# Opening fillers, five groups of squares, a reordered even mixer and shorter boundary sums in a two-layer decoder trunk

## The chip, the cores and the metric

The kernel runs on one core of one Trainium2 chip, in one launch. The metric is device time in microseconds (us). Five engines work beside each other and are tied by semaphores: PE (TensorE, matrix products), DVE (VectorE), ACT (ScalarE), POOL (GpSimd) and SP (SyncE, which here only starts transfers). Each runs its own instructions strictly in the order in which they stand in its program, so an instruction that waits holds up all that stand behind it on that engine.

## The reference, cut to what matters

A trunk of two layers over 512 tokens of width 1024, conditioned by a vector `c`. Layer 0 has the even mixer (sliding-window attention and a Conformer convolution side by side), layer 1 a state-space mixer. Each mixer and each feed-forward block is preceded by an RMS norm and a modulation, so that the sum of squares over the width of `x` is needed at the start, at three places between blocks, and at the end.

```
silu_c = silu(c)
for i in range(2):
    sh_m, sc_m, g_m, sh_f, sc_f, g_f = split(silu_c @ w_mod[i] + b_mod[i], 6)
    h = rmsnorm(x, norm_mix[i]) * (1 + sc_m) + sh_m
    y = even_mixer(h, ...) if i == 0 else ssd_mixer(h, ...)
    x = x + g_m * y
    h = rmsnorm(x, norm_ffn[i]) * (1 + sc_f) + sh_f
    x = x + g_f * ((silu(causal_conv(h @ w_gate)) * (h @ w_val)) @ w_down)
return rmsnorm(x, final_norm)          # x * rsqrt(mean(x*x) + eps) * g
```

In the even mixer, `q`, `k`, `v` and the convolution's input are `h @ w_in + b_in`; `q` and `k` are rotated by angles worked out from `positions`; the attention's and the convolution's outputs are joined and multiplied by `w_out`.

## The kernel before, in words

`x` lies transposed: eight tiles of 128 channels (`kt`), each 128 partitions by 512 tokens. Every fp32 product is made as three products of rounded halves (`mm3`, L370 to L372): high by high, low by high, high by low. So a weight tile is cast on ACT to its high part (`head`, L317 `wh`) and its remainder is subtracted on DVE (`rest`, L322 `wl`); the weights of the first projection that share the opening have their own cast (L753, `wg_head`) and remainder (L757, `wg_rest`), and the activation `hn` likewise an `upper` part (L790, ACT) and a `lower` one (L794, DVE).

**Opening.** The eight tiles of `x` are squared on ACT (L693). DVE adds the first seven squares into one tile (`x_add`, L696), and PE sums that tile and the eighth square over the partitions by products with a column of ones (`x_sum`, L702, four products of one column for each tile). PE also spreads constants (L404) and runs ten filler products, `warm` (L672). The root (ACT L728), Newton's step (DVE L425 to L429) and a spread of the result (`x_row`, L404) follow; then the first tile of `hn` is made, and `begin` (L798) starts the first projection, six banks wide, with `hh`, `hl` and `lh` products for each `kt` as the tiles come. The modulation's dot products run on DVE meanwhile (`mod_dot`, L595, an operation of 128x1024). POOL works out the rotary angles (L1279 on), and then starts eight small transfers.

**Even mixer.** The rest of the projection (eight column tiles of 24 products each), the Conformer's convolution as PE products (L950), scores (mask L1041 and L1048), the transposes of the probabilities (L1090), their copies to SBUF on ACT (L1097, `bring`), the products with V (L1108) and the products with `w_out` are all tasks of one plan. A list scheduler orders them by the length of the chain behind a task plus a weight from a table by the task's name (`MIXER0`); the result is a fixed order on every engine.

**Boundary.** The function that closes a block works in two halves of 256 tokens (`hf` 0 and 1). For each output tile: products, `residual` (DVE L474), its square on ACT (L501), and, as long as more tiles follow, an addition of an older square into `acc` on DVE (L499). When the last tile of half 0 is done, `W.ahead()` prepares one weight tile of the next block (cast on ACT, remainder on DVE), and `norm_steps` sums `acc` and the squares that were not yet added by products with ones (L396: six products of 128x1 for a half), then takes the root (ACT L508) and Newton's step (DVE L510 to L516). There are four such places: after the even mixer, after each feed-forward block and after the state-space mixer; the last one has no weight left to prepare, and `final` multiplies and writes the output.

Of the kernel before, what the change touches and what calls it, by code (L numbers as in the profile page):

```python
# [24 lines left out]
P = 128  # L25
# [45 lines left out]
WARM = 10  # L71
# [7 lines left out]
MIXER0 = {'sigmoid': 150, 'square': -128, 'osq_add': -45, 'head': 130, 'tap0': -113, 'attn_h': 63, 'conv_h': -48, 'out_c': -99, 'gated': -114, 'rest': -119, 'values': 58, 'rope': 138, 'rstd': -10, 'mod_sum': 7, 'attn_l': 143, 'var': 124, 'turn': -64, 'mod_end': -110, 'exp': -57, 'bring': -43, 'conv_sum': 54, 'out_a': -120, 'osq': 8, 'mod_act': -104, 'mod_add': 39, 'mod_free': 120, 'normalize': 150, 'load': -64, 'product': -72, 'mean_row': -150, 'mod_dve': 105, 'tap': -30, 'recip': -56, 'ln': -15, 'centre': -64, 'residual': 71, 'maxima': 147, 'rstd_row': 38, 'conv_l': -16, 'mean': 47, 'rope_in': 128, 'v_bias': 31, 'mod_load': -56, 'mod_dot': -129, 'root': -125, 'rows': -16, 'rows_in': 47, 'v_turn': -18, 'v_in': 45, 'mod 2': -83, 'head 0': 40, 'mu': 146, 'keys': -96, 'conv 0': 150, 'head 1': -134, 'mod 1': -150, 'head 3': -150, 'shifts': -98, 'scores': -50, 'mod 0': 117, 'conv 3': -14, 'conv 2': 11, 'cbias': 86, 'conv': 82, 'store': 86, 'taps': 79, 'conv 1': 84, 'head 2': -150, 'wg_load': 80, 'c_row': -142, 'norm': 96, 'hl': -96, 'x_newton': -58, 'preload': 145, 'others': -120, 'wg_head': 62, 'finish': 115, 'sines': 150, 'v_load': -81, 'first 4': 88, 'upper': 126, 'wg_rest': 138, 'hh': -129, 's_gain': 79, 'first 2': -68, 'widen': -150, 'x_load': 72, 'x_root': -38, 'x_add': -61, 'x_total': -33, 's_dot': 38, 'lh': 105, 'x_sq': 80, 'masks': 73, 't_turn': 145, 'c_in': -110, 'ss_load': -128, 'first 5': -56, 'gain': 115, 'w_free': -14, 'normed': 104, 'margins': -50, 'side': -136, 'x_row': 146, 'first 0': 11, 'h_dot': 129, 't_in': -51, 'first 1': -141, 'first 6': -43, 'angles': -150, 'first 3': -16, 'lower': 49, 'first 7': -17, 'h_bias': 25, 'x_sum': -40, 'late': -140, 'late0': 65, 'csum': 55, 'warm': -93, 'p_dot': 70, 'p_in': 4, 'p_sum': 43, 'mean_in': 100}  # L79
# [145 lines left out]
def trunk(ctx: ExitStack, tc: tile.TileContext, xT_d, vecs_d, rows_d, dsk_d, pos_d, const_d, wss_d, wg0_d,  # L225
# [250 lines left out]
    def boundary(ws, ms, acts, gate, acc, nxt, after=None):  # L476
# [28 lines left out]
        def norm_steps(hf):  # L505
            s_ = token_sums([acc[:, HALF[hf]], *sq[hf]], 2)
            sd, v, y_, a, y2 = (small(2) for _ in range(5))
            act(sd, s_, AF.Sqrt, scale=1.0 / 1024.0, bias=eps[:, 0:1])  # L508
            yield
            ts(v, s_, 1.0 / 1024.0, 1e-6, ALU.mult, ALU.add)  # L510
            nc.vector.reciprocal(y_, sd)
            tt(a, y_, y_, ALU.mult)
            yield
            stt(a, a, -0.5, v, ALU.mult, ALU.mult)
            yield
            stt(y2, a, 1.5, y_, ALU.add, ALU.mult)  # L516
            yield
            y[hf] = spread(y2, 2)
# [126 lines left out]
    def even_layer(lp, cp, dp0):  # L645
# [49 lines left out]
        def x_add(k):  # L695
            tt(st["xq", 0], st["xq", 0], st["xq", k], ALU.add)  # L696
# [8 lines left out]
        sums = None  # L705
# [104 lines left out]
        for kt in range(KT):  # L810
# [5 lines left out]
            wl_ = add("wg_rest", "DVE", 0.93, lambda kt=kt: wg_rest(kt), [wh_], None, dict(raw=1))  # L816
# [1001 lines left out]
    def final(fp):  # L1818
        def fill(hf, rb):
# [144 lines left out]
```

## Time and profile before

| | |
|---|---|
| median of 3 runs | 1341.47 us (1340.62 to 1342.1) |
| the profiled execution | 1342.0 us |
| its span, first to last instruction | 1340.2 us |
| PE busy | 1313.2 us, 98% of the span |
| DVE, ACT, POOL busy | 875.1, 597.0, 74.7 us |
| mean granted TensorE clock | 0.990 |
| share of PE in the chain that ended last | 93% |

The profile has a page for the whole execution (busy time of each engine, the span in forty slices, the chain of work that ended last, the costliest groups) and views of a stretch: a timeline of single instructions or runs of like ones, a table of busy times and granted clock by stretch, and the waits of one engine. A granted clock of 1.00 is 2.4 GHz and 0.50 is 1.2 GHz. An instruction is named by its line in the kernel before.

### The profile page before, as it was taken

Reading aid. Unit: us, or ns where it says so; the run is one execution under the profiler, and the core shown is the slowest. Engines: PE = TensorE matmul, PEld = TensorE weight load, DVE = VectorE, ACT = ScalarE, POOL = GpSimd, SP = SyncE. Lnnn points to the kernel's source line nnn. Section 1 sums busy time; section 2 is a strip of 40 time slices with the busy share of each in tenths; the row PEclk is TensorE's granted clock in tenths of the full one; section 3 lists DMA queues with packets and bytes.
Section 4 is the critical chain, followed back from the end, with each engine's and each line's share of the span. In section 5 each row is a group of like instructions: output and inputs, shape, how many; then the busy total and the mean of one; then the engine's idle time right before and its main releaser. Section 6 shows DMA issues by size and latency. Waiting matters only on the chain.

```text
span 1340.2 us, 17613 instructions
## 1 busy us (share of the span) xinstructions
PE 1313.2 (98%) x6873; PEld 1078.0 (80%) x6873; DVE 875.1 (65%) x1342; ACT 597.0 (45%) x947; POOL 74.7 (6%) x129
## 2 busy tenths in 40 slices
PE   7999899999999999999999999999999999999997
PEld 6856589888888888897888887887988888888886
DVE  6976987775666676568686775878665434434443
ACT  4624734432233233347694764836353313322333
POOL 7010000000000000100110100000000000000002
PEclk8999899999999999999999999999999999999999
DMA  9773363564664665223542432342223233233311
GB/s 341 236 266 103 128 210 111 170 222 152 215 194 149 218 203 180 89 68 95 166 139 84 139 110 97 122 123 79 64 94 115 89 111 94 83 92 112 99 56 63
DMA packets 56436, 183.64 MB, mean 137 GB/s; under 512 B 7008, under 2 KB 10144, under 8 KB 56352
## 3 DMA queue, kind: packets, MB, share of 16 engines
q1 hardware_dynamic: 51536, 170.24, 39.5%
q0 software_dynamic: 4128, 11.61, 2.6%
q8 instruction: 54, 0.88, 0.3%
q10 hardware_dynamic: 688, 0.66, 0.1%
q14 instruction: 30, 0.25, 0.1%
HBM read 179.21 MB, written 3.28 MB: 136 GB/s over the span
## 4 chain that ended last, share of the span: by engine, by line
PE 93%; DVE 3%; ACT 2%; DMA 1%; issue 1%; DVEq 0%; ACTq 0%; POOLq 0%
PE ps L370 27%; PE ps L371 27%; PE ps L372 27%; PE ps L798 2%; PE ps L950 2%; PE ps L1643 1%; DMA M<-scr 1%; PE ps L1621 1%; PE ps L404 1%; PE ps L396 1%; PE ps L1609 1%; ACT M L1593 0%; PE ps L419 0%; PE ps L1108 0%; PE ps L1635 0%
## 5 line engine op out<-in xcount | busy, mean ns | idle before, releaser
L370 PE MATMUL ps<-hn,wh 128*128 128x512 f32 (+1 forms) x1214 | 460.2, 379 | 0.8 <-ACT hn L461 0.8
L371 PE MATMUL ps<-hn,wh 128*128 128x512 f32 (+1 forms) x1214 | 454.1, 374 | 0.4
L372 PE MATMUL ps<-hn,wl 128*128 128x512 f32 (+1 forms) x1214 | 453.9, 374 | 0.0
L322 DVE TENSOR_TENSOR wl<-raw,wh 128x1024 fp32r<-128x1024 f32 (+1 forms) x208 | 250.9, 1209 | 95.1 <-ACT wh L317 93.8
L317 ACT CAST wh<-raw 128x1024 fp32r<-128x1024 f32 (+1 forms) x208 | 213.1, 1027 | 221.5 <-PE ps L371 216.1
L370 PEld LDWEIGHTS ps<-hn,wh 128*128 128x128 f32 x1214 | 228.5, 188 | 44.6 <-issue 3.5
L371 PEld LDWEIGHTS ps<-hn,wh 128*128 128x128 f32 x1214 | 228.7, 188 | 42.3 <-issue 1.9
L372 PEld LDWEIGHTS ps<-hn,wl 128*128 128x128 f32 x1214 | 228.5, 188 | 40.7
L474 DVE SCALAR_TENSOR_TENSOR x<-ps,modv,x 128x512 f32<-128x512 f32 (+1 forms) x108 | 73.9, 690 | 115.2 <-PE ps L372 115.2
L370 PE MATMUL ps<-fh,wh 128*128 128x512 f32 (+1 forms) x380 | 142.2, 374 | 0.0
L371 PE MATMUL ps<-fl,wh 128*128 128x512 f32 (+1 forms) x380 | 141.9, 373 | 0.0
L372 PE MATMUL ps<-fh,wl 128*128 128x512 f32 (+1 forms) x380 | 141.9, 373 | 0.0
L595 DVE SCALAR_TENSOR_TENSOR mr<-mr,cb 128x1024 f32<-128x1024 f32 x92 | 111.1, 1219 | 1.6 <-DMA mr<-in_wmod_dram 1.6
L1346 ACT ACTIVATE tmp<-ps,vecs 128x512 f32<-128x512 f32 x44 | 34.2, 777 | 114.8 <-PE ps L372 114.8
L1347 DVE SCALAR_TENSOR_TENSOR tmp<-ps,vecs,tmp 128x511 f32<-128x511 f32 x44 | 32.9, 749 | 79.6 <-ACT tmp L1346 79.6
L370 PEld LDWEIGHTS ps<-fh,wh 128*128 128x128 f32 x380 | 71.5, 188 | 12.8
L372 PEld LDWEIGHTS ps<-fh,wl 128*128 128x128 f32 x380 | 71.5, 188 | 12.7
L371 PEld LDWEIGHTS ps<-fl,wh 128*128 128x128 f32 x380 | 71.5, 188 | 12.6
L295 ACT CAST fh<-tmp 128x512 fp32r<-128x512 f32 x44 | 27.3, 620 | 96.4 <-DVE tmp L1351 95.6
L449 POOL TENSOR_TENSOR ssq<-ssq,tmp 128x512 f32<-128x512 f32 x10 | 13.4, 1337 | 909.8 <-ACT tmp L448 909.8
L1349 ACT ACTIVATE tmp<-tmp 128x512 f32<-128x512 f32 x44 | 27.8, 632 | 75.6 <-DVE tmp L1348 75.5
L1593 ACT ACTIVATE M<-M,acs 128x128 f32<-128x128 f32 x128 | 39.6, 389 | 24.4 <-DMA M<-scr 24.3
(291 smaller groups left out, 1462.1 us busy)
## 6 DMA issues: line engine op xcount, KB each, us to landing
raw<-in_w_dram SPq DMA_DIRECT2D x176, 512.0 KB, 3.7
mr<-in_wmod_dram SPq DMA_DIRECT2D x80, 512.0 KB, 3.7
raw<-in_w_dram SPq DMA_DIRECT2D x32, 448.0 KB, 3.4
mr<-in_wss_dram SPq DMA_DIRECT2D x16, 512.0 KB, 7.2
M<-scr POOLq DMA_DIRECT2D x16, 512.0 KB, 4.6
s<-uc SPq DMA_DIRECT2D x16, 266.0 KB, 5.2
raw<-in_wg_dram SPq DMA_DIRECT2D x8, 384.0 KB, 7.5
E<-scr POOLq DMA_DIRECT2D x32, 96.0 KB, 3.7
```

What stands on the lines that cost most here:

```text
L295: nc.scalar.copy(h, src)
L317: nc.scalar.copy(h, self.raw[i].rearrange("p (k m) -> p k m", m=P))
L322: eng.tensor_tensor(l, self.raw[i].rearrange("p (k m) -> p k m", m=P), h.bitcast(F32), ALU.subtract)
L370: mm(ps, lhsT=w[0], rhs=ah, start=first, stop=False)
L371: mm(ps, lhsT=w[0], rhs=al, start=False, stop=False)
L372: mm(ps, lhsT=w[1], rhs=ah, start=False, stop=last)
L474: stt(x[:, m, hs], ps, gate(m), x[:, m, hs], ALU.mult, ALU.add)
L595: stt(raw, raw, 1.0, mod_pool[2], ALU.mult, ALU.mult, accum_out=out)
L1346: act(c, pg, AF.Identity, bias=vec("fcb", i), scale=vec("fcw", 3 * i + 2))
L1347: stt(c[:, 1:], pg[:, :T - 1], vec("fcw", 3 * i + 1), c[:, 1:], ALU.mult, ALU.add)
L1349: act(c, c, AF.Silu)
L1593: act(m_[:, i, c, :], m_[:, i, c, :], AF.Relu, bias=acs[:, c, h:h + 1], scale=-1.0)
```

## The change

It has seven parts.

1. Eight filler products (`warm`), now of a column of ones with itself, stand at the head of PE's program; seven more stand between the sums of the squares, and the first `hh` product waits for all of them.
2. The squares of `x` are summed on PE in five groups (tile 0; tile 1; tiles 2 to 5, which DVE adds with three additions; tile 6; tile 7) instead of two, so twenty one-column products instead of eight, and three additions instead of six.
3. The angles on POOL are held until the upper part of tile 4 of `hn` is there, by a small copy from it that POOL makes first.
4. The opening's remainders (`wg_rest`) may go to DVE or to POOL.
5. The table `MIXER0` has other weights, so that the whole even mixer is ordered anew.
6. `norm_steps` adds left-over squares into `acc` on DVE first, until none is left in half 0 and one in half 1: two products with ones in half 0 and four in half 1, instead of six in each.
7. The last output transfers leave from other queues: the last tile's from ACT's instead of SP's, and the first pair of tiles of the second half goes one step earlier.

The core of the diff (the table's numbers are left out, the order below tells what they do):

```diff
-WARM = 10
+WARM, EARLY = 7, 8
+ANGLES_AT = 4
...
         def norm_steps(hf):
+            while len(sq[hf]) > hf:
+                tt(acc[:, HALF[hf]], acc[:, HALF[hf]], sq[hf].pop(0), ALU.add)
             s_ = token_sums([acc[:, HALF[hf]], *sq[hf]], 2)
...
+        filler = ones.broadcast_to([P, P])
         def warm():
-            mm(g0[NG0 - 1][:, 0:P], lhsT=ident, rhs=con[:, :P], start=True, stop=True)
+            mm(g0[NG0 - 1][:, 0:P], lhsT=filler, rhs=filler, start=True, stop=True)
+        for _ in range(EARLY):
+            warm()
...
         def x_add(k):
-            tt(st["xq", 0], st["xq", 0], st["xq", k], ALU.add)
+            tt(st["xq", 2], st["xq", 2], st["xq", k], ALU.add)
...
-            if k == 0:
-                sums = t
-            elif k < KT - 1:
-                sums = add("x_add", "DVE", 0.69, lambda k=k: x_add(k), [t, sums], None, dict(tmp=1))
-            else:
-                sums = add("x_sum", "PE", 1.0, lambda: x_sum(0), [sums], dict(ps=1), dict(tmp=1))
+            if 2 < k < 6:
+                added = add("x_add", "DVE", 0.69, lambda k=k: x_add(k), [t, added], None, dict(tmp=1))
+            if k == 2:
+                added = t
+            elif k in (0, 1):
+                sums = add("x_sum", "PE", 1.0, lambda k=k: x_sum(k), [t, sums], None if k else dict(ps=1), dict(tmp=1))
+            elif k == 5:
+                sums = add("x_sum", "PE", 1.0, lambda: x_sum(2), [added, sums], None, dict(tmp=1))
+            elif k > 5:
                 sums = add("x_sum", "PE", 1.0, lambda k=k: x_sum(k), [t, sums], None, dict(tmp=1))
+        warms = []
         for _ in range(WARM):
-            add("warm", "PE", 0.45, warm, cbs)
+            warms.append(add("warm", "PE", 0.45, warm, [], bonus=-400))
...
-            wl_ = add("wg_rest", "DVE", 0.93, lambda kt=kt: wg_rest(kt), [wh_], None, dict(raw=1))
+            wl_ = plan.either("wg_rest", [Way("DVE", 0.93, lambda kt=kt: wg_rest(kt, nc.vector)),
+                                          Way("POOL", 1.75, lambda kt=kt: wg_rest(kt, nc.gpsimd))],
+                              [wh_], None, dict(raw=1))
...
-                hh = add("hh", "PE", 1.39, lambda kt=kt: begin(kt, 0, 0), [wh_, h_, begun])
+                hh = add("hh", "PE", 1.39, lambda kt=kt: begin(kt, 0, 0), [wh_, h_, begun, *(() if kt else warms)])
-                angles_at = hh if kt == 2 else angles_at
+                angles_at = h_ if kt == ANGLES_AT else angles_at
...
         def angle():
+            nc.gpsimd.tensor_copy(small(8), hn[ANGLES_AT][0][:, 0:8].bitcast(F32))
...
                 tt(o[:, kt % 2, :], x[:, kt, hs], rb, ALU.mult)
+                if hf and n == 5:
+                    nc.scalar.dma_start(out_d[:, 0:2, hs], os_[0])
                 if hf and n > 3:
-                    nc.sync.dma_start(out_d[:, kt:kt + 1, hs], o[:, kt % 2:kt % 2 + 1, :])
+                    (nc.scalar if n == 5 else nc.sync).dma_start(out_d[:, kt:kt + 1, hs], o[:, kt % 2:kt % 2 + 1, :])
...
-            nc.scalar.dma_start(out_d[:, 0:2, hs], os_[0])
+            if not hf:
+                nc.scalar.dma_start(out_d[:, 0:2, hs], os_[0])
```

How the order changes, at three places (lines of the changed kernel stand a few higher: L672 becomes L676, L702 L709, L404 L405, L774 L785, L322 L323, L474 L475).

PE at its start, before: two spreads of constants (`con`), ten fillers, two groups of sums (`ones,tmp`).

```order
L404 MATMUL ps_134<-con 128x128 x4
L404 MATMUL ps_144<-con 128x128 x4
L672 MATMUL ps_126<-con 128x128 x10
L702 MATMUL ps_194<-ones,tmp_139 128x1 x4
L702 MATMUL ps_194<-ones,tmp_178 128x1 x4
L774 MATMUL ps_208<-mr_169,con 32x128 x8
L404 MATMUL ps_237<-con,sm_225 128x128 x4
```

PE at its start in the changed kernel:

```order
L676 MATMUL ps_126<-ones 128x128 x8
L405 MATMUL ps_142<-con 128x128 x4
L405 MATMUL ps_152<-con 128x128 x4
L709 MATMUL ps_162<-ones,tmp_147 128x1 x4
L676 MATMUL ps_126<-ones 128x128
L709 MATMUL ps_162<-ones,tmp_150 128x1 x4
L676 MATMUL ps_126<-ones 128x128 x3
L709 MATMUL ps_162<-ones,tmp_159 128x1 x4
```

Fillers now stand ahead of everything and between the sums. Two more groups follow (`tmp_188`, `tmp_193`), each behind one filler, then L785 as before, the last filler, and the spread of the root.

DVE at the first boundary, half 0, before: residuals (L474), additions of squares (L499), the remainder of the weight tile that is prepared ahead (L322), Newton's step (L510 on).

```order
L474 SCALAR_TENSOR_TENSOR x<-ps_2024,modv,x 128x256
L499 TENSOR_TENSOR ssq_129<-ssq_129,tmp_2022 128x256
L474 SCALAR_TENSOR_TENSOR x<-ps_2041,modv,x 128x256
L322 TENSOR_TENSOR wl_2066<-raw_2057,wh_2065 128x1024
L510 TENSOR_SCALAR sm_2106<-ps_2098 128x2
L511 RECIPROCAL sm_2107<-sm_2105 128x2
```

The same place in the changed kernel:

```order
L475 SCALAR_TENSOR_TENSOR x<-ps_2040,modv,x 128x256
L500 TENSOR_TENSOR ssq_137<-ssq_137,tmp_2038 128x256
L475 SCALAR_TENSOR_TENSOR x<-ps_2057,modv,x 128x256
L323 TENSOR_TENSOR wl_2082<-raw_2073,wh_2081 128x1024
L508 TENSOR_TENSOR ssq_137<-ssq_137,tmp_2055 128x256
L508 TENSOR_TENSOR ssq_137<-ssq_137,tmp_2071 128x256
L513 TENSOR_SCALAR sm_2120<-ps_2116 128x2
```

The two new additions (L508) stand behind the remainder, and PE's two products with ones (L397, which read `ssq_137`) wait for the second of them. The second and third boundary read the same.

POOL behind its first memsets, before: the angles follow at once.

```order
L653 MEMSET zeros 128x30
L662 MEMSET s_117 128x512
L662 MEMSET s_119 128x512
L1279 CAST sm_392<-pos 128x4
L1282 ISA
L1282 TENSOR_TENSOR ang_394<-sm_392,invf 128x32
```

POOL in the changed kernel:

```order
L656 MEMSET zeros 128x30
L665 MEMSET s_117 128x512
L665 MEMSET s_119 128x512
L768 ISA
L768 TENSOR_TENSOR wl_233<-raw_205,wh_232 128x768
L768 TENSOR_TENSOR wl_318<-raw_288,wh_317 128x768
L768 TENSOR_TENSOR wl_410<-raw_373,wh_409 128x768
L887 COPY sm_441<-hn_438 128x8
L1293 CAST sm_443<-pos 128x4
```

Three remainders (of tiles 0, 2 and 4) and the holding copy now stand ahead of the angles.

## Rows read from the trace of the kernel before

**Rows 1.** The page: busy time by engine; share of the chain that ended last.
```profile
PE 1313.2 (98%) x6873; PEld 1078.0 (80%) x6873; DVE 875.1 (65%) x1342; ACT 597.0 (45%) x947; POOL 74.7 (6%) x129
...
PE 93%; DVE 3%; ACT 2%; DMA 1%; issue 1%; DVEq 0%; ACTq 0%; POOLq 0%
```

**Rows 2.** PE's waits: for whom; total us, times, longest.
```profile
PE ps L1108 <- ACT s L1097: 4.1, 3, 3.3
PE ps L1643 <- DVE M L1600: 3.5, 3, 1.7
```

**Rows 3.** Timeline of PE, opening: start, us, engine, line, operands, [idle before, releaser].
```profile
4.63 3.78 PE L404 MATMUL ps<-con 128*128 128x128 f32 x16 [4.63 <-ACT con L657]
8.21 3.20 PE L672 MATMUL ps<-con 128*128 128x128 f32 x20
13.82 1.95 PE L702 MATMUL ps<-ones,tmp 128*128 128x1 f32 x16 [2.42 <-DVE tmp L696]
...
17.00 2.08 PE L404 MATMUL ps<-con,sm 128*128 128x128 f32 x8 [0.66 <-DVE sm L429]
...
21.26 2.93 PE L798 MATMUL ps<-hn,wh 128*128 128x512 f32 x6 [0.96 <-ACT hn L790]
...
24.27 2.86 PE L798 MATMUL ps<-hn,wl 128*128 128x512 f32 x6
...
27.63 1.67 PE L798 MATMUL ps<-hn,wh 128*128 128x512 f32 x6
```

**Rows 4.** Windows: PE, PEld, DVE, ACT, POOL busy, granted clock, DMA share, GB/s.
```profile
20.00:25.00 5.00, 4.04 (x18) 3.06 (x11) 3.44 (x5) 1.92 (x6) 4.31 (x10) 0.50 1.03 405
152.00:154.00 2.00, 0.14 (x2) 0.00 (x0) 2.00 (x4) 1.09 (x2) 0.00 (x0) 1.00 0.85 281
164.00:166.00 2.00, 2.00 (x6) 1.57 (x5) 2.00 (x3) 2.00 (x12) 0.00 (x0) 0.50 0.05 8
...
900.00:910.00 10.00, 8.33 (x52) 6.69 (x51) 3.89 (x5) 9.08 (x22) 0.32 (x1) 1.00 0.27 78
```

**Rows 5.** Opening's last square (ACT), remainder (DVE line), a POOL addition, sines (ACT).
```profile
6.73 4.07 ACT L693 ACTIVATE tmp<-x 128x512 f32<-128x512 f32 x6 [0.99 <-DMA x<-in_xT_dram]
...
L757 DVE TENSOR_TENSOR wl<-raw,wh x8: 946/958/965, 16.9 to 47.8; 128x768 fp32r<-128x768 f32 x8
...
L449 POOL TENSOR_TENSOR ssq<-ssq,tmp x10: 1286/1298/1535, 554.1 to 1318.9; 128x512 f32<-128x512 f32 x10
...
65.20 0.35 ACT L878 ACTIVATE ang<-ang 128x32 f32<-128x32 f32 x2
```

**Rows 6.** Timeline of PE at the attention's end.
```profile
145.21 1.13 PE L1048 MATMUL ps<-s,s 64*128 64x256 f32 x8
...
155.48 1.15 PE L1108 MATMUL ps<-s,s 128*64 128x128 f32 x12 [3.34 <-ACT s L1097]
...
157.90 2.08 PE L1048 MATMUL ps<-s,s 64*128 64x256 f32 x8
```

**Rows 7.** Timeline of ACT, PE and DVE, first boundary; the addition's line, min/median/max ns.
```profile
211.69 1.03 ACT L317 CAST wh<-raw 128x1024 fp32r<-128x1024 f32 x1
...
212.00 0.50 PE L396 MATMUL ps<-ones,ssq 128*128 128x1 f32 x4
...
212.75 1.23 DVE L322 TENSOR_TENSOR wl<-raw,wh 128x1024 fp32r<-128x1024 f32 x1 [1.48 <-ACT wh L317]
...
213.26 0.37 PE L370 MATMUL ps<-s,wh 128*128 128x256 f32 x1
...
L499 DVE TENSOR_TENSOR ssq<-ssq,tmp x8: 415/418/426, 208.3 to 963.0; 128x256 f32<-128x256 f32 x8
```

**Rows 8.** Timeline of the tail: DVE's outputs, last issues of ACT and SP.
```profile
1333.24 2.08 DVE L1828 TENSOR_TENSOR o<-x,ps 128x256 f32<-128x256 f32 x6 [1.21 <-ACT rs L1822]
...
1334.72 0.44 ACTq L1834 DMA_DIRECT2D out_dram<-o  x1
1335.15 1.52 SPq L1830 DMA_DIRECT2D out_dram<-o  x2
```

More of the change, by code (lines that the diff above doesn't have):

```diff
@@ L78 @@
 N_S = 26
-MIXER0 = {'sigmoid': 150, 'square': -128, 'osq_add': -45, 'head': 130, 'tap0': -113, 'attn_h': 63, 'conv_h': -48, 'out_c': -99, 'gated': -114, 'rest': -119, 'values': 58, 'rope': 138, 'rstd': -10, 'mod_sum': 7, 'attn_l': 143, 'var': 124, 'turn': -64, 'mod_end': -110, 'exp': -57, 'bring': -43, 'conv_sum': 54, 'out_a': -120, 'osq': 8, 'mod_act': -104, 'mod_add': 39, 'mod_free': 120, 'normalize': 150, 'load': -64, 'product': -72, 'mean_row': -150, 'mod_dve': 105, 'tap': -30, 'recip': -56, 'ln': -15, 'centre': -64, 'residual': 71, 'maxima': 147, 'rstd_row': 38, 'conv_l': -16, 'mean': 47, 'rope_in': 128, 'v_bias': 31, 'mod_load': -56, 'mod_dot': -129, 'root': -125, 'rows': -16, 'rows_in': 47, 'v_turn': -18, 'v_in': 45, 'mod 2': -83, 'head 0': 40, 'mu': 146, 'keys': -96, 'conv 0': 150, 'head 1': -134, 'mod 1': -150, 'head 3': -150, 'shifts': -98, 'scores': -50, 'mod 0': 117, 'conv 3': -14, 'conv 2': 11, 'cbias': 86, 'conv': 82, 'store': 86, 'taps': 79, 'conv 1': 84, 'head 2': -150, 'wg_load': 80, 'c_row': -142, 'norm': 96, 'hl': -96, 'x_newton': -58, 'preload': 145, 'others': -120, 'wg_head': 62, 'finish': 115, 'sines': 150, 'v_load': -81, 'first 4': 88, 'upper': 126, 'wg_rest': 138, 'hh': -129, 's_gain': 79, 'first 2': -68, 'widen': -150, 'x_load': 72, 'x_root': -38, 'x_add': -61, 'x_total': -33, 's_dot': 38, 'lh': 105, 'x_sq': 80, 'masks': 73, 't_turn': 145, 'c_in': -110, 'ss_load': -128, 'first 5': -56, 'gain': 115, 'w_free': -14, 'normed': 104, 'margins': -50, 'side': -136, 'x_row': 146, 'first 0': 11, 'h_dot': 129, 't_in': -51, 'first 1': -141, 'first 6': -43, 'angles': -150, 'first 3': -16, 'lower': 49, 'first 7': -17, 'h_bias': 25, 'x_sum': -40, 'late': -140, 'late0': 65, 'csum': 55, 'warm': -93, 'p_dot': 70, 'p_in': 4, 'p_sum': 43, 'mean_in': 100}
@@ new lines @@
+MIXER0 = {'sigmoid': -63, 'square': -119, 'osq_add': 26, 'head': 8, 'tap0': -113, 'attn_h': -111, 'conv_h': -120, 'out_c': 95, 'gated': 139, 'rest': -129, 'values': 150, 'rope': 15, 'rstd': -106, 'mod_sum': 7, 'attn_l': 132, 'var': 52, 'turn': -66, 'mod_end': 76, 'exp': -150, 'bring': 13, 'conv_sum': 54, 'out_a': -32, 'osq': 4, 'mod_act': -104, 'mod_add': 39, 'mod_free': 120, 'normalize': 43, 'load': 106, 'product': -18, 'mean_row': -119, 'mod_dve': 105, 'tap': -30, 'recip': 73, 'ln': 5, 'centre': -41, 'residual': -24, 'maxima': 133, 'rstd_row': -115, 'conv_l': -83, 'mean': 47, 'rope_in': 88, 'v_bias': 47, 'mod_load': 0, 'mod_dot': -40, 'root': -37, 'rows': 63, 'rows_in': -14, 'v_turn': -40, 'v_in': 116, 'mod 2': -66, 'head 0': -85, 'mu': 74, 'keys': -150, 'conv 0': 138, 'head 1': -129, 'mod 1': -95, 'head 3': -149, 'shifts': -20, 'scores': 140, 'mod 0': -76, 'conv 3': -150, 'conv 2': 135, 'cbias': 86, 'conv': 44, 'store': 24, 'taps': 62, 'conv 1': 91, 'head 2': -144, 'wg_load': 50, 'c_row': 5, 'norm': -86, 'hl': -16, 'x_newton': 150, 'preload': 65, 'others': -121, 'wg_head': -74, 'finish': -141, 'sines': 44, 'v_load': 3, 'first 4': 65, 'upper': 17, 'wg_rest': -133, 'hh': -59, 's_gain': -123, 'first 2': 19, 'widen': -146, 'x_load': 97, 'x_root': 21, 'x_add': -61, 'x_total': -33, 's_dot': 63, 'lh': 81, 'x_sq': 5, 'masks': -102, 't_turn': 13, 'c_in': -145, 'ss_load': -110, 'first 5': 116, 'gain': 144, 'w_free': 14, 'normed': -73, 'margins': -67, 'side': -44, 'x_row': 138, 'first 0': -6, 'h_dot': 28, 't_in': -89, 'first 1': -123, 'first 6': 99, 'angles': -150, 'first 3': 97, 'lower': -67, 'first 7': -18, 'h_bias': 93, 'x_sum': -32, 'late': -6, 'late0': 49, 'csum': -20, 'warm': 74, 'p_dot': -100, 'p_in': -14, 'p_sum': 55, 'mean_in': -58}
@@ L753, in wg_head, with wg_rest @@
             nc.scalar.copy(st["w", kt][0], st["wg", kt])
-        def wg_rest(kt):
+        def wg_rest(kt, engine):
             h, l = st["w", kt]
-            tt(l, st["wg", kt], h.bitcast(F32), ALU.subtract)
+            engine.tensor_tensor(l, st["wg", kt], h.bitcast(F32), ALU.subtract)
         def scale(kt):
```

2 lines of the change are left out of this document (1 added, 1 removed).

## The prediction

> **What bounds the kernel now.** I read the page first: PE is busy for 98% of the span and carries 93% of the chain that ended last [rows 1]. So a change counts only where PE stands idle, where it runs at 1.2 GHz instead of 2.4, or where its work grows. The view of PE's waits says how little that is: one wait of 3.34 us in the attention, five short ones in the second mixer (3.5 in all, which this change leaves alone) [rows 2], and the opening. The timeline and the windows give the rest. In the opening PE has its first product at 4.63, is idle for 2.42 before the sums at 13.82, and begins the projection (L798) at 21.26 [rows 3]; the granted clock there is 0.50 (20 to 25), and a spread of constants at 17.00 takes 2.08 for eight records [rows 3, 4], so the clock had fallen by then. At the attention's end PE is nearly empty from 152 to 154 and then gets 0.50 until about 166: the scores at 157.90 take 2.08 instead of 1.13 [rows 4, 6].
>
> **Opening.** The eight early fillers need only a memset of DVE's, which is done at about 1.1 us, so PE starts some 3.5 us earlier. The spreads of constants took 3.78 us for sixteen records of 128x128, 0.236 each, and the twenty filler records behind them 0.160 on average [rows 3]: the clock was low at first. Eight fillers are sixteen such records, so at 0.236 they fill the time from 1.1 up to 4.9, when the constants come; they cost nothing. If the clock rises half-way through the spreads, these end near 7.8 instead of 8.41 (between 4.9 + 3.78 = 8.7 and 4.9 + 16 x 0.160 = 7.5). The sums are now five groups: sixteen records took 1.95, so eight take 0.98 and five groups 4.9. The last square is there at 6.73 + 4.07 = 10.80 [rows 5], and DVE's third addition near 10.0, so PE does not wait for its data any more: from 7.8 on, 4.9 of sums and about 1.9 of fillers end at about 14.6, against 13.82 + 1.95 = 15.77. That is 1.2 us, less than the idle that disappears, because twelve more products (24 records, 2.9 us) take its place. Root and Newton's step are as before; the spread of the result (2.08 at the lower clock [rows 3], about half at the higher) and the first upper part follow, and `hh` starts at about 18.6 with the higher clock all along, or 19.9 with the lower, against 21.26. The lower clock before cost the first two groups of products 2.93 and 2.86 where a group later took 1.67 of record time, a spacing of 1.4 [rows 3]: 5.7 us at half rate, so 2.8 lost. **With the clock kept, the opening gains 2.7 + 2.8 = 5.5; if the clock falls again in the sums, 1.4, and some of the 2.8 since the dense work starts sooner: about 2.** One-column products did not hold the clock before (the fall came with the sums at 13.82 or right behind them [rows 3]); now a third of that time is fillers. I take 4.0, between the two and nearer the first.
>
> The remainders that move to POOL take three times 0.96 us from DVE [rows 5]; on POOL each takes about 1.95, an estimate from 1.30 for 128x512 against 128x768. Their products (`lh`) come later than `hh` and `hl`, 2.8 us behind, so POOL hides them. Were it late, PE would wait up to 1 us for the first. The angles are about 24 us of POOL work; held until about 32 they end at 56, and their reader, ACT's sines, ran at 65.20 [rows 5]: no cost, with 9 us in hand. The three additions of squares less free DVE of 2 us early, which nobody waits for.
>
> **Even mixer.** Between the first mixer products and 183 us PE's work is the same before and after, only its order differs; what can be won is idle time and slow time. Idle: 3.34 plus two short waits, 4.1 [rows 2]. Slow: the scores at 157.90 took 2.08 where the same took 1.13 at 145.21 [rows 6], the products with V the same 0.9 more, and the products with `w_out` up to about 166.9 run 4.4 us at half rate [rows 4], 2.2: together 4.0. So 8.1 is the most. The new order puts products with `w_out` between the last heads, but at the end the transposes of one head, ACT's copies and the products with V still follow each other; by the copies (about 0.6 each, four to six for a head) a wait of 1.5 to 2 us stays there, and if the clock falls again most of the slow time stays too. The other bound is below nothing: the new order also puts the convolution's last shifted loads and DVE's copies of V behind other work, each good for a wait of 1 to 3 us. I take 4.0 from a range of -8 to +3, half of what there is to win.
>
> **Boundaries.** Before, the first boundary's sums start at 212.00 and the next product at 213.26: 1.26 us for six products, with no wait, since `acc` and both squares are ready [rows 7]. After, two products need both new additions, and these stand on DVE behind the remainder of the weight tile, which waits for ACT's cast (211.69 + 1.03 = 212.72) and runs from 212.75 to 213.98 [rows 7]. Then two additions of 0.42 [rows 7]: 214.82. PE's sums begin at 214.85 instead of 212.00, take 0.4 for two products, and the next product comes at 215.3 instead of 213.26: **2.0 us lost, at three boundaries** (the other two begin at 577.88 and 957.76 with the same rows), 6.0. Nothing else stands in PE's order to fill the wait, and PE is what all later work waits for. In half 1 two products less save 0.4, and the one addition (0.42) ends about when the last square does, so 0.3 three times: -0.9. The fourth boundary has no weight tile; its additions end before the root's table is loaded: nothing. So +5.1 at an unchanged clock.
>
> A PE that stands still for 2.8 us may also lose its clock. The nearest rows: 3.34 idle was followed by 0.50 [rows 4, 6]; the second mixer's waits of at most 1.7 [rows 2] lie at 1.00, as from 900 to 910 with 1.7 idle [rows 4]. The price of one fall is 0 to 4 (the 4.0 above), in dense work that resumes at once rather 2. Three places, bounds 0 to 12; I take 1.7, about one fall.
>
> The Trainium skill ("TensorE: Matmul & The Clock Gate", Part 1) says that the unit that watches TensorE's activity runs freely and not in step with the kernel, so that the same kernel meets it at another phase in each run. By that the same stall could lower the clock at one boundary and not at the next; the trace has the fall after 3.34 and none after 1.7, and nothing between, so it neither confirms nor denies it here.
>
> **Tail.** DVE's last output is done at 1333.24 + 2.08 = 1335.32, and SP issues the last transfers from 1335.15 for 1.52 [rows 8]; after, SP has one and ACT, free since 1335.16, has the other: 0.5 us (0 to 0.9). The Trainium skill ("DMA: Bandwidth & Descriptors", Issuing engines are not separate DMA queues) says that transfers from several issuing engines share the same sixteen DMA engines, so only issue time is saved; that is how the 0.5 is counted, and no run here shows more.
>
> **The sum.** Opening -4.0, even mixer -4.0, boundaries +5.1 and +1.7, tail -0.5: -1.7 us against the profiled execution of 1342.0, so 1340.3. That execution is 0.5 above the median of the runs, 1341.47; on the median's level it is 1339.8. I say 1340.0. A measurement of this kernel can tell about 0.2%, 2.7 us, from no change.
>
> **Rivals.** *Larger gain, 1333.5:* the fillers keep the clock (-5.5), the even mixer gains 6.5, the stalls leave the clock alone: -5.5 - 6.5 + 5.1 - 0.5 = -7.4, on the median's level 1334.1. For it: a third of the sums' time is now dense, and the reordering aims PE's products at the empty place. Against: the chain of transposes, copies and V stays. *The stall does not come, 1330:* if DVE reached the additions before the remainder, or PE had other work there, the boundaries would gain 0.8 + 0.4 three times, 3.6, and the sum be -4.0 - 4.0 - 3.6 - 0.5 = -12.1. Against it: both orders are fixed. *The stalls take the clock, 1348:* at all three boundaries the clock falls, 4 us each: -4.0 - 4.0 + 5.1 + 12 - 0.5 = +8.6, 1350; with 2 us each +2.6, 1344. It decides for slower once the three falls cost more than about 6 us. *A fed even mixer, 1346:* PE comes earlier than DVE's and the queues' work can follow, the 4.0 there turns into +2: +4.3. That the change does not do what it says (opening clock falls, nothing won in the mixer) gives -2 + 6.8 - 0.5 = +4.3 as well.
>
> **How the numbers follow.** Forecast, within 0.2%: 0.36, its own range 1337 to 1344. Larger gain 0.28 and no stall 0.10: together 0.38 faster. Stalls that take the clock 0.12, a fed mixer or an opening that gains little 0.14: 0.26 slower. The range reaches from the larger gain, with part of the no-stall case, to the middle of the slower cases: 1331 to 1347.
>
> **What would show it.** Right: PE idle of some 2.8 us before L397 at about 205, 570 and 950, released by DVE's L508; `hh` (L809) starting at 18.6 to 20; a granted clock of 1.00 from 15 to 25 if the opening's larger value holds; less than 2 us of idle before L1122 products. Wrong: no wait before L397, or PE's wait there shorter than 1.5; an `hh` later than 21; new waits of PE on DVE or transfers between 70 and 180; windows of 0.50 behind a boundary would raise the price to the third rival's.

## The result, and the profile after

The changed kernel takes 1350.14 us (median of 4, 1348.17 to 1351.01), the kernel before 1341.78 in the same comparison (1340.62 to 1342.6): a ratio of 1.0061, 95% interval 1.0043 to 1.0078. That is slower by 0.6%, clear of noise; 1340.0 was forecast, with a range of 1331 to 1347. In all comparisons together the kernel before ran from 1337.8 to 1343.98, so one profile beside another proves nothing below some 3 us, and medians and intervals carry the verdicts here. The experiments were timed in three comparisons on different chips, in which the median of the kernel before was 1341.44, 1340.66 and 1341.01, so medians from two of them can be set beside each other to about 1 us only; each ratio is to the kernel before of the same comparison.

The page of the changed kernel shows PE as busy as before, and a smaller share of PE in the chain that ended last, 87% instead of 93% [rows 1]: DVE, ACT, DMA and POOL now hold it up in places.

```profile
span 1349.2 us, 17588 instructions
...
PE 1316.1 (98%) x6859; PEld 1083.0 (80%) x6859; DVE 878.6 (65%) x1348; ACT 595.6 (44%) x946; POOL 84.7 (6%) x133
...
PE 87%; DVE 4%; ACT 3%; DMA 2%; POOL 2%; issue 1%; SPq 0%; DVEq 0%; ACTq 0%; POOLq 0%
```

PE's waits in the changed kernel (for whom; total us, times, longest) answer [rows 2]. The first line is new: three of its five waits are those at the first three boundaries, a fourth of 1.26 stands in the second half of the last one. The opening's wait for the constants and the attention's wait of 3.34 are gone, and five small ones have come.

```profile
PE ps L397 <- DVE ssq L508: 9.5, 5, 2.7
PE ps L1657 <- DVE M L1614: 4.4, 3, 2.4
PE ps L964 <- DMA s<-uc: 1.6, 1, 1.6
PE ps L1062 <- DVE s L1017: 1.3, 1, 1.3
...
PE ps L1136 <- DVE sm L1091: 1.0, 1, 1.0
...
PE ps L1034 <- ACT tmp L1029: 0.8, 1, 0.8
...
PE ps L1122 <- DVE s L1038: 0.8, 1, 0.8
```

The timeline of the first boundary answers [rows 7]. The remainder (L323) runs from 207.65, the two additions (L508) behind it, and PE has been idle for 2.66 us when its sums start. The other two boundaries read the same, with 2.73 and 2.64 (last two lines).

```profile
206.59 1.03 ACT L318 CAST wh<-raw 128x1024 fp32r<-128x1024 f32 x1
207.64 1.28 ACT L511 ACT_TABLE_LOAD   x1
207.65 1.23 DVE L323 TENSOR_TENSOR wl<-raw,wh 128x1024 fp32r<-128x1024 f32 x1 [1.48 <-ACT wh L318]
208.79 0.88 DVE L508 TENSOR_TENSOR ssq<-ssq,tmp 128x256 f32<-128x256 f32 x2
...
209.72 1.01 PE L397 MATMUL ps<-ones,ssq 128*128 128x1 f32 x4 [2.66 <-DVE ssq L508]
...
580.50 0.58 PE L397 MATMUL ps<-ones,ssq 128*128 128x1 f32 x4 [2.73 <-DVE ssq L508]
...
966.09 0.60 PE L397 MATMUL ps<-ones,ssq 128*128 128x1 f32 x4 [2.64 <-DVE ssq L508]
```

Windows of the changed kernel behind the first boundary, behind the second, and in the second mixer (PE, PEld, DVE, ACT, POOL busy, granted clock, DMA share, GB/s) show that each standstill is followed by a stretch at 0.50.

```profile
205.00:210.00 5.00, 2.34 (x20) 2.14 (x18) 2.56 (x5) 2.84 (x4) 0.00 (x0) 0.95 0.12 7
210.00:215.00 5.00, 5.00 (x24) 5.00 (x25) 1.93 (x8) 1.09 (x3) 0.00 (x0) 0.50 0.25 98
215.00:220.00 5.00, 4.43 (x30) 4.03 (x30) 3.08 (x8) 1.83 (x4) 0.00 (x0) 0.87 0.15 31
...
580.00:582.00 2.00, 1.50 (x11) 1.53 (x12) 0.88 (x5) 0.26 (x1) 0.00 (x0) 0.88 0.71 166
582.00:584.00 2.00, 2.00 (x11) 2.00 (x11) 0.68 (x3) 0.42 (x1) 0.00 (x0) 0.50 0.27 104
584.00:586.00 2.00, 2.00 (x16) 2.00 (x15) 0.66 (x2) 0.15 (x1) 0.00 (x0) 0.77 0.00 0
...
910.00:912.00 2.00, 0.00 (x0) 0.00 (x0) 1.28 (x2) 2.00 (x6) 0.00 (x0) 1.00 0.00 0
912.00:914.00 2.00, 2.00 (x18) 1.58 (x19) 0.92 (x2) 2.00 (x6) 0.00 (x0) 0.65 0.00 0
914.00:916.00 2.00, 2.00 (x6) 1.60 (x5) 1.97 (x4) 2.00 (x4) 0.00 (x0) 0.50 0.01 4
```

How long a stretch lasts follows from the mean clock: a window at 0.88 of 2 us had 0.48 us at half rate. Behind the first boundary that makes 0.5 + 5.0 + 1.3 = 6.8 us at half rate, behind the second 0.5 + 2.0 + 0.9 = 3.4; the third (966 to 972) and the place in the second mixer read like the second. In dense work half of that is lost: 3.4, 1.7, 1.7 and 1.7.

Put stage by stage, by when PE reaches the sums of half 0 (start of the sums less the idle before them; in the filled kernel the start of the fillers), this is where the time went. The last two columns are experiments told of below.

| us of PE's time | before | after | after, stall filled | additions ahead |
|---|---|---|---|---|
| start to first boundary | 212.0 | 207.1 | 206.3 | 207.3 |
| first to second | 365.9 | 370.7 | 367.7 | 365.2 |
| second to third | 379.9 | 385.7 | 382.3 | 379.9 |
| third to fourth | 365.9 | 369.2 | 367.9 | 365.1 |
| fourth to end of span | 16.5 | 16.5 | 17.1 | 16.7 |

The opening and the even mixer gained 4.9 us. The three stages that begin with one of the first three boundaries lost 4.8, 5.8 and 3.3, together 13.9. The second of them also holds the second mixer, with its wait of 2.44 and the slow stretch behind it.

### The profile page after: what moved, and what is told of

Read it like the earlier page. It is cut to its first block, busy times and chain, and to the rows that moved or that the text cites. A ratio compares the mean times of both kernels' runs of the same rounds, so it can differ in the third digit from the quotient of the medians.

```text
span 1349.2 us, 17588 instructions
## 1 busy us (share of the span) xinstructions
PE 1316.1 (98%) x6859; PEld 1083.0 (80%) x6859; DVE 878.6 (65%) x1348; ACT 595.6 (44%) x946; POOL 84.7 (6%) x133
## 4 chain that ended last, share of the span: by engine, by line
PE 87%; DVE 4%; ACT 3%; DMA 2%; POOL 2%; issue 1%; SPq 0%; DVEq 0%; ACTq 0%; POOLq 0%
PE ps L371 26%; PE ps L372 26%; PE ps L373 26%; PE ps L964 2%; DMA M<-scr 1%; PE ps L1657 1%; DVE mr L598 1%; PE ps L1635 1%; PE ps L809 1%; PE ps L1623 1%; ACT M L1607 1%; PE ps L397 0%; PE ps L405 0%; DMA s<-uc 0%; ACT wh L318 0%
## 5 line engine op out<-in xcount | busy, mean ns | idle before, releaser
L323 DVE TENSOR_TENSOR wl<-raw,wh 128x1024 fp32r<-128x1024 f32 (+1 forms) x208 | 250.9, 1209 | 90.7 <-ACT wh L318 89.7
L475 DVE SCALAR_TENSOR_TENSOR x<-ps,modv,x 128x512 f32<-128x512 f32 (+1 forms) x108 | 74.0, 689 | 121.7 <-PE ps L373 121.7
L450 POOL TENSOR_TENSOR ssq<-ssq,tmp 128x512 f32<-128x512 f32 x10 | 13.4, 1336 | 911.5 <-ACT tmp L449 911.5
L296 ACT CAST fh<-tmp 128x512 fp32r<-128x512 f32 x44 | 27.3, 620 | 96.4 <-DVE tmp L1365 96.4
```

What stands on the lines that cost most here:

```text
L296: nc.scalar.copy(h, src)
L323: eng.tensor_tensor(l, self.raw[i].rearrange("p (k m) -> p k m", m=P), h.bitcast(F32), ALU.subtract)
L475: stt(x[:, m, hs], ps, gate(m), x[:, m, hs], ALU.mult, ALU.add)
```

## The experiments

Theory A: the loss is PE's wait behind the additions at three boundaries, and the clock that falls behind each. Rival B: the loss is made by the new order of the even mixer or in the second mixer. Rival C: the additions cost wherever they stand. Rival D: the stalls alone make the loss.

**Without the boundary part.**

```diff
         def norm_steps(hf):
-            while len(sq[hf]) > hf:
-                tt(acc[:, HALF[hf]], acc[:, HALF[hf]], sq[hf].pop(0), ALU.add)
             s_ = token_sums([acc[:, HALF[hf]], *sq[hf]], 2)
```

> The changed kernel without its boundary part: the squares left over are again summed by PE (six products with ones in each half), all else as changed. Theory A (the loss is PE's wait at the first three boundaries, 2.66, 2.73 and 2.64 us in the trace of after, and the clock that falls behind each): the waits and the three stretches at 0.50 behind them are gone and the lead of 4.9 us that the changed kernel has before the first boundary stays, so about 1341.8 - 4.9 = 1336.9 us (1335 to 1339). Rival B (the loss is in the new order of the even mixer or in the second mixer, and the boundaries only show it): 1345 or more. Whether the fall of the clock at 912 in the second mixer goes too is open: 1336.9 if so, about 1339.3 if not.

1339.39 us (1337.82 to 1341.82, 10 runs), ratio to before 0.999, interval 0.998 to 1.000. 10.8 us of the changed kernel's time go with this one part, so B falls. Its profile has no stretch at 0.50 from 24 to 1330, so the fall in the second mixer is gone too (its longest wait there is 1.81). The time is 2.5 above what was expected, and just outside the range. The profile is at 208.3 at the first boundary and not at 207.1, and 0.8 of these 1.2 us arose in the opening, where no instruction was changed: there the first `hh` took 2.93 instead of 1.65, and the first projection's products ended at 52.81 instead of 52.01. So the lead of 4.9 in the one profile of after was not that of every execution.

**The boundary part alone, on the kernel before.** The same two lines are added to the kernel before.

> The kernel before with the boundary part alone (left-over squares added on DVE first). Theory A: three waits of 2.7 us less what the shorter sums save, 5 us, and three falls of the clock at 1.7 to 3.4 us each, 5 to 10: 1352 us (1348 to 1356). If the stalls cost but the clock mostly stays: 1347. Rival B: 1341.8, within 1.

1353.37 us (1351.3 to 1353.62, 4 runs), ratio 1.0089, interval 1.0068 to 1.011: 12 us slower, in the expected range. Its profile has waits of 2.66, 2.73 and 2.64 us at the three boundaries, as after, and a stretch at half rate behind each. This is the first, in the timeline of PE and in windows:

```profile
213.58 0.61 PE L396 MATMUL ps<-ones,ssq 128*128 128x1 f32 x4 [2.66 <-DVE ssq L507]
...
212.00:214.00 2.00, 0.42 (x4) 0.42 (x4) 1.49 (x3) 0.77 (x1) 0.00 (x0) 1.00 0.35 33
214.00:216.00 2.00, 2.00 (x15) 2.00 (x15) 1.11 (x6) 0.44 (x2) 0.00 (x0) 0.80 0.60 229
216.00:218.00 2.00, 2.00 (x12) 2.00 (x11) 0.82 (x2) 0.66 (x2) 0.00 (x0) 0.50 0.00 0
```

**The stall filled with work, the sums where they are.** Ten products of ones go into the sums' own bank right before them, at the first three boundaries.

```diff
-    def token_sums(srcs, n=NCH):
+    def token_sums(srcs, n=NCH, fillers=0):
-        ps = bank((P, n))
+        ps = bank((P, P if fillers else n))
+        for _ in range(fillers):
+            mm(ps[:, 0:P], lhsT=ones.broadcast_to([P, P]), rhs=ones.broadcast_to([P, P]), start=True, stop=True)
...
-        return ps
+        return ps[:, 0:n]
...
-            s_ = token_sums([acc[:, HALF[hf]], *sq[hf]], 2)
+            s_ = token_sums([acc[:, HALF[hf]], *sq[hf]], 2, 10 if nfirst and not hf else 0)
```

> The changed kernel with ten filler products of ones put on PE right before the sums of half 0 at the first three boundaries, into the same bank, so that PE is at work (some 2.4 us) while it waits for DVE. The place of the sums doesn't move, only the clock can differ. Theory A with the clock as half of the loss: no stretch at 0.50 behind a boundary, about 1341.8 - 4.9 + 5.2 = 1342.1 us (1341 to 1345). Rival D (the stalls alone make the loss, the clock's falls are hidden): 1349 to 1351 as before.

1345.15 us (1342.34 to 1350.53, 10 runs), ratio to before 1.0037, interval 1.0023 to 1.0051. That is just above the 1341 to 1345 that were expected. The sums still start 2.8 us after PE reaches the place, but the clock stays, in this profile at 1.00 from 20 to 1331. Timeline of PE and windows behind the first boundary:

```profile
206.26 2.39 PE L396 MATMUL ps<-ones 128*128 128x128 f32 x20
...
209.08 0.61 PE L399 MATMUL ps<-ones,ssq 128*128 128x1 f32 x4 [0.43 <-DVE ssq L510]
...
205.00:210.00 5.00, 4.57 (x41) 4.38 (x40) 2.47 (x4) 2.90 (x4) 0.00 (x0) 1.00 0.16 40
210.00:215.00 5.00, 4.58 (x40) 4.37 (x38) 3.73 (x13) 1.90 (x5) 0.00 (x0) 1.00 0.17 68
```

So work that computes nothing makes the kernel 5 us faster, and D falls. By the table the stalls cost 1.8, 2.4 and 2.0 us, 6.3 in all before rounding. The rest of the 13.9, 7.6 us in this pair of profiles and 5.0 between the medians, goes with the clock. Not all of the 7.6 stands behind the boundaries: the changed kernel's fall in the second mixer, worth 1.7, is missing in the filled kernel, whose longest wait there is 1.7, so that about 6 are left for the three boundaries.

**Four fillers instead of ten.**

```diff
-            s_ = token_sums([acc[:, HALF[hf]], *sq[hf]], 2, 10 if nfirst and not hf else 0)
+            s_ = token_sums([acc[:, HALF[hf]], *sq[hf]], 2, 4 if nfirst and not hf else 0)
```

> As the kernel with the filled stall (e4), with four fillers instead of ten at each of the first three boundaries, so that PE works about 1 us and then stands still for some 1.7 us in one piece. If the clock falls only after a standstill of more than about 2 us, as the waits of the second mixer suggest (1.8 and less without a fall, 1.9 to 3.0 with one in the profiles so far), no stretch at 0.50 stands behind the boundaries and the time is that of e4, 1345 us (1343 to 1346.5). If any stall of that kind lowers it, 1349 to 1351 as the changed kernel.

1345.34 us (1343.68 to 1348.47, 9 runs), ratio 1.0032, interval 1.0021 to 1.0043: the time of ten. In its profile PE stands still for about 1.8 us in one piece, and the clock fell behind one of the three boundaries, the second; behind the third it stayed:

```profile
576.38 0.58 PE L399 MATMUL ps<-ones,ssq 128*128 128x1 f32 x4 [1.84 <-DVE ssq L510]
...
576.00:578.00 2.00, 1.62 (x10) 1.65 (x11) 0.84 (x6) 0.26 (x1) 0.00 (x0) 0.78 0.74 211
578.00:580.00 2.00, 2.00 (x11) 2.00 (x11) 0.58 (x2) 0.42 (x1) 0.00 (x0) 0.50 0.13 51
...
960.00:962.00 2.00, 1.72 (x14) 1.72 (x15) 0.90 (x7) 0.26 (x1) 0.00 (x0) 1.00 0.78 190
```

So a standstill of 1.8 us may or may not cost the clock, and the expectation that below 2 us it does not was too simple. The profiles of all thirteen kernels together, from 30 us to 1315, say more: of the 35 waits of PE from 1.0 to 1.71 us that their timelines show none was followed by a stretch at 0.50, of the ten from 1.75 to 1.95 two were (this one of 1.84, and one of 1.90 in the kernel with POOL as before, but not the longest, 1.95), and of the 18 from 2.12 to 3.34 every one was.

**The additions ahead of the weight tile, on the changed kernel.**

```diff
         for i in range(len(ws)):
             finish(0, i, products(0, i))
+        while sq[0]:
+            tt(acc[:, HALF[0]], acc[:, HALF[0]], sq[0].pop(0), ALU.add)
         W.ahead()
         norm0 = norm_steps(0)
```

> The changed kernel with the two additions of half 0 put ahead of the preparation of the next weight tile, so that on DVE they stand before the remainder instead of behind it; the sums keep their two products. Theory A: PE's wait before the sums shrinks to under 0.5 us, no stretch at 0.50 behind a boundary, and the shorter sums save some 0.5 us a boundary: 1335 to 1336 us, 1 to 2 below the kernel without boundary additions. Rival C (the additions themselves, not their place, make PE wait): waits of over 1 us stay and the time is 1342 or more.

1337.48 us (1334.02 to 1340.26, 10 runs), ratio to before 0.9972, interval 0.9961 to 0.9984. It beats both kernels. It is above the 1335 to 1336 that were expected, but 1.9 below the kernel without the boundary part, as expected, and no stretch at 0.50 stands between 20 and 1325. The timeline of its first boundary shows the same instructions in the other order: the second addition waits 0.21 for ACT's square, PE waits for nothing that the view shows, and the remainder starts where it started, since it waits for ACT's cast anyway.

```profile
206.16 0.41 DVE L526 TENSOR_TENSOR ssq<-ssq,tmp 128x256 f32<-128x256 f32 x1
...
206.67 1.03 ACT L318 CAST wh<-raw 128x1024 fp32r<-128x1024 f32 x1
206.79 0.42 DVE L526 TENSOR_TENSOR ssq<-ssq,tmp 128x256 f32<-128x256 f32 x1 [0.21 <-ACT tmp L502]
...
207.27 0.61 PE L397 MATMUL ps<-ones,ssq 128*128 128x1 f32 x4
...
207.73 1.23 DVE L323 TENSOR_TENSOR wl<-raw,wh 128x1024 fp32r<-128x1024 f32 x1 [0.51 <-ACT wh L318]
```

**The same on the kernel before.** The kernel before with the boundary part and the additions ahead, nothing else.

> The kernel before with the boundary part alone, its two additions of half 0 ahead of the preparation of the next weight tile. Theory A: no wait over 0.5 us before the sums at the first three boundaries, 0.5 us saved at each and 0.3 in half 1: 1339 to 1340.3, against 1353.4 with the additions behind the remainder. Rival C (additions on DVE in this place cost whatever their place): 1342 or more.

1338.93 us (1338.24 to 1340.48, 10 runs), ratio 0.9987, interval 0.9978 to 0.9997, against 1353.37 with the additions behind the remainder: some 14 us hang on the place of six instructions. In its profile PE waits at most 0.2 before the sums of half 0 at the first three boundaries. C falls. Shorter sums are worth some 2 us when they stand in the right place, here and on the changed kernel (1339.39 to 1337.48).

**The opening's fillers left out.** In the kernel with the additions ahead the filler task issues nothing, so that every other instruction stands in the same order.

```diff
         def warm():
-            mm(g0[NG0 - 1][:, 0:P], lhsT=filler, rhs=filler, start=True, stop=True)
+            pass
```

> The kernel with the additions ahead (e3) with every filler of the opening left out of PE's program, while all other instructions of all engines keep their order (the kernel without fillers, e6, had its whole mixer ordered anew by the planner and so didn't tell). Theory A, the fillers raise the clock before the first sums and shorten its second fall: PE starts at 4.6, the first hh at 20.5 to 21.5, shared products end 1.5 to 3 us later than 51.5: 1339 to 1340.5. Rival (fillers do nothing, the five groups make the lead): 1337.5, end of the shared products at 51.5 within 0.5.

1341.54 us (1339.18 to 1343.56, 10 runs), ratio 1.0001, interval 0.999 to 1.0011: in this order of tasks the fillers are worth about 4 us, more than the 1.5 to 3 expected. Timeline of PE, first without fillers, where five groups of sums in one piece take 8.53 us and the first `hh` takes 2.93:

```profile
4.74 3.79 PE L405 MATMUL ps<-con 128*128 128x128 f32 x16 [4.74 <-ACT con L662]
8.32 8.53 PE L711 MATMUL ps<-ones,tmp 128*128 128x1 f32 x40
...
21.89 2.93 PE L811 MATMUL ps<-hn,wh 128*128 128x512 f32 x6 [0.51 <-ACT hn L803]
...
24.89 2.75 PE L811 MATMUL ps<-hn,wl 128*128 128x512 f32 x6
```

and then with them, where `hh` starts 2.0 us earlier and runs at full rate:

```profile
1.15 3.78 PE L678 MATMUL ps<-ones 128*128 128x128 f32 x16 [1.15 <-DVE eps L282]
...
6.90 0.95 PE L711 MATMUL ps<-ones,tmp 128*128 128x1 f32 x8
...
19.86 1.65 PE L811 MATMUL ps<-hn,wh 128*128 128x512 f32 x6 [0.60 <-ACT hn L803]
```

The durations say why. Without fillers a record of the sums takes 0.213 us (8.53 for 40), where with them the first group's take 0.119 (0.95 for 8), and `hh` and the products behind it take 2.93 and 2.75, as they took 2.93 and 2.86 before at a granted clock of 0.50 [rows 3, 4]. So PE ran at half rate from its first product on, and its trace has the first change of the clock, a rise, at 27.3. The windows show 1.00 for all the time before, because the trace's record of the clock begins with that change; there one has to go by the durations. With fillers the trace has the rise at 5.4, a fall at 12.2 and the next rise at 19.0, just before `hh`.

The first projection's shared products end (read off the start of the next product) at 56.03 without and at 51.53 with fillers. Before they ended at 54.92, so without fillers the changed opening, with its five groups, is the longer one in these profiles. Each is one execution: in the profiles of three other kernels with these fillers `hh` still took 2.93, and in the kernel with `WARM, EARLY = 0, 0` below, also without fillers, it took 1.66. The 4 us are the medians'.

**Parts taken back that reorder the rest.** Four kernels let the planner order the mixer anew, because the set of tasks or the table changed.

> The kernel before with the opening's fillers and the five groups of squares alone (old table of weights, angles at once, all remainders on DVE, old boundaries). Theory A, by the stage times of the profiles: the first projection's last shared products end 2 to 3.4 us earlier and nothing else changes, the wait of 3.3 us and the slow stretch in the attention stay: 1338.5 us (1337.5 to 1340). Rival E (the opening's lead is taken back, since DVE and the transfers behind it can't follow without the new table): within 1 us of before.

The kernel before with the opening's fillers and groups alone (WARM, EARLY, `x_add` and `x_sum` as in the diff of the change): 1343.97 us (1339.88 to 1346.0, 10 runs), ratio 1.002, interval 1.0007 to 1.0033. Slower, where 1338.5 was expected. Its profile reaches the first boundary at 208.6, 3.4 us ahead of before, and loses it again in the second mixer with a wait of 3.0 us and a fall of the clock there. That the median is above before is not explained by it.

> The kernel with the additions ahead (e3) without any filler product, five groups of squares kept. If the fillers hold the clock or raise it sooner, the first hh product starts later than in e3 (19.9) or runs at 0.50: the shared products end 2 to 3 us later than 51.5, and the time is 1339.5 to 1340.5. If the fillers do nothing (the groups alone make the lead), 1337.5 as e3, with the same start of hh.

With `WARM, EARLY = 0, 0` on the kernel with the additions ahead: 1348.58 us (1347.28 to 1349.87), ratio 1.0053 (4 runs). It reaches the first boundary at 215.0, so the mixer took 161.7 us from the end of the shared products (53.36) instead of 155.7: a worse order, not the fillers' worth.

> The kernel with the additions ahead (e3) with the old MIXER0 table: what the new order of the even mixer is worth. Theory A, by the stage times of the profiles (end of the shared products to the first boundary's sums: 157.1 us before, 155.1 to 155.7 with the new table): 1.4 to 2 us, so about 1339 us, with the wait of 3 us in front of the products with V and the stretch at 0.50 behind it back. Rival F (the table is worth more, since without it the opening's lead is lost too): 1341 or more.

With the old `MIXER0`: 1348.42 us (1345.61 to 1348.67), ratio 1.0047 (4 runs), 161.7 us from 55.03 to 216.72. As expected the attention's wait (3.1 us) and the stretch at 0.50 are back, but the loss is about 11 us and not 1.4 to 2: the old table orders the new set of tasks worse than it did the old one (157.1).

> The kernel with the additions ahead (e3) with POOL as before: angles at once, all eight remainders of the opening on DVE. My prediction counted these two parts at nothing: 1337.5, within 1 us of e3. If three remainders on POOL do take load from DVE that PE waits for, the shared products end later than 51.5 (by up to 1.5 us) and the time is 1338.5 to 1339.

With POOL as before (`wg_rest` on DVE alone, the angles not held): 1341.27 us (1337.73 to 1343.38, 10 runs), ratio 0.9996, 3.8 above the kernel with the additions ahead. The shared products end at 50.89, earlier than 51.53, so POOL's parts win nothing in the opening that this profile shows; the mixer, ordered anew, takes 159.5 instead of 155.7.

These four are 3 to 11 us above the kernels that they were made from, which suggests that a table of weights is tuned to one set of tasks. They can't say what each part is worth by itself, and that stays open for the five groups, POOL's parts and the table.

## Why the prediction was wrong

**The stall: right.** The prediction named the place, the order on DVE and the 2.8 us (2.85 by its rows). PE waited 2.66, 2.73 and 2.64, and net of the shorter sums a boundary cost 1.8 to 2.4, where 2.0 was worked out; the fourth boundary cost nothing, as said, although PE waits 1.26 there.

**The clock behind the stall: the step that failed.** The prediction had it as "I take 1.7, about one fall", with bounds of 0 to 12. It fell at all three boundaries, in the changed kernel and in the kernel with the boundary part alone, so six times of six after 2.6 to 2.7 us, and a fourth time in the second mixer after a wait of 2.44. The term measured 5.0 us between medians and 7.6 between profiles, about 6 of these at the boundaries; the second mixer, which the prediction held untouched by the change, made the rest. The rival "the stalls take the clock" described this and had 12 chances in 100. The sum was right in kind and the count wrong: the rows had a fall after 3.34 and none after 1.7, and 2.7 was closer to the first. With three falls instead of one, at its own 1.7 to 2 each, the forecast would have been 1.7 to 2.6 slower than before. (The five short waits of the second mixer that it reads from [rows 2] are three; nothing hangs on that.)

The Trainium skill ("TensorE: Matmul & The Clock Gate", Part 1) says that the watch on TensorE runs freely, not in step with the kernel. At 2.7 us the traces show no such choice, since each stall was followed by a fall. Like stalls did differ in how long the slow stretch lasted (behind 2.66 us at the first boundary 6.8 us in the changed kernel, 3.4 in the kernel with the boundary part alone), and at 1.8 us in whether the clock fell at all (one of three). That fits the sentence, but no run here shows that this is the reason.

**The opening: -4.0 forecast, -2.9 measured** (shared products end at 52.01 instead of 54.92). PE began at 1.15 and reached `hh` at 20.39 instead of 18.6 to 19.9. The step that failed is the middle value: the clock did fall in the sums, as the windows of the changed kernel show, so that the last two groups took 1.71 each where 0.98 was worked out. And PE did wait for its data, 0.98 us for DVE's third addition. What the prediction had for a fall in the sums, about 2, is a little nearer. The dense work then ran at full rate from the first `hh` on, since the slow stretch was over; the timeline row at 20.39 answers the one at 21.26 in [rows 3]. (The prediction lets the products with the remainders, `lh`, come behind `hh` and `hl`; in [rows 3] they come right behind `hh`. PE lost only 0.3 us to a remainder, one of DVE's.) Timeline of PE, windows from 12 to 18, and the timeline again:

```profile
10.31 1.05 PE L709 MATMUL ps<-ones,tmp 128*128 128x1 f32 x8 [0.98 <-DVE tmp L703]
...
13.69 1.71 PE L709 MATMUL ps<-ones,tmp 128*128 128x1 f32 x8
...
12.00:14.00 2.00, 2.00 (x11) 2.00 (x11) 1.23 (x2) 0.26 (x2) 0.00 (x0) 0.50 1.03 412
14.00:16.00 2.00, 2.00 (x23) 1.90 (x23) 0.25 (x2) 0.57 (x2) 0.00 (x0) 0.50 1.01 403
16.00:18.00 2.00, 2.00 (x16) 1.67 (x9) 0.48 (x3) 0.96 (x3) 1.50 (x1) 0.50 1.04 408
...
20.39 1.65 PE L809 MATMUL ps<-hn,wh 128*128 128x512 f32 x6 [1.05 <-ACT hn L801]
```

**The even mixer: -4.0 forecast, -2.0 measured** (4.9 less 2.9). It went another way than supposed. The new waits that the prediction gave as a sign of being wrong came, and PE's idle time did not shrink: the waits listed above from L964 to L1122, with one of 0.4, make 5.9 us between 52 and 207 against 4.1 before. But none is longer than 1.6, and no stretch at 0.50 follows: the windows from 150 to 205 all stand at 1.00. So the gain comes from the slow stretch, worth some 4 us before, that is no more.

**The tail: -0.5 forecast, 0 measured.** DVE's last output to the end of the span is 4.88 us before (1335.32 to 1340.2) and 4.87 after. The last issue ended 1.35 us after DVE's last output before, and 0.40 after, so the issue did get shorter and nothing followed from it: in both kernels the DMA engines are busy at a share of 1.0 for three us behind DVE's last output (1335 to 1338 and 1344 to 1347). The Trainium skill ("DMA: Bandwidth & Descriptors", Issuing engines are not separate DMA queues) says that only issue time is saved; here not even that reached the end.

**In sum** -2.9 - 2.0 + 6.3 + 7.6 + 0 = +9.0 us between the two profiled spans (1340.2 and 1349.2), against -1.7. Of the 10.7 between them the clock's term makes 5.9, the opening and the even mixer 3.1, the stalls 1.2 and the tail 0.5. The clock alone, had the rest come as forecast, would have made it +4.2, slower instead of faster.

**Left open.** Why the wait of the second mixer varies between kernels whose order there is the same (its longest is 1.5 to 3.0 us, with a fall of the clock in some), why the clock of the opening differs between profiles with the same opening, and how much of the spread of the runs, several us, comes from these two.

## What to carry to other kernels

Work that is moved off the bound engine still counts if that engine waits for it: look at what stands ahead of it in the other engine's order, and emit what the bound engine waits for before any work that is prepared for later. Price a standstill of TensorE by its length plus the slow stretch behind it, here behind none of the waits up to 1.71 us, two of the ten from 1.75 to 1.95 and all from 2.12 on, and if it can't be avoided, fill it with products into a bank that is free. A tuned order belongs to the tasks that it was tuned for, so take a part back inside the same order (a task that issues nothing) rather than by changing the set of tasks.

## What the runs showed of the hardware

That filler products which compute nothing take 5 us off the time when they stand in three stalls of 2.7 us, though PE does not start the next useful product any sooner. That no wait of PE up to 1.71 us was followed by 1.2 GHz, two of ten from 1.75 to 1.95 us were, and all 18 from 2.12 to 3.34 us, in the stages between opening and tail of thirteen profiles. That the stretch at 1.2 GHz behind like stalls lasted 3.4 us in two places and 6.8 in a third. And that at the start PE could be at work from 4.7 us on and still stay at half rate until 27.3, in the one profile without the opening's fillers that is shown above.
